# Two-layer gMLP and attention encoder on one core: later maxima transposes, one post step per key tile, bias copies on ScalarE, second weight low halves on GpSimd

## The chip, the cores and the metric

The kernel runs on one core of a Trainium2 chip. The metric is the device time of one execution in microseconds, the median of three runs. Five engines work side by side, each through its own row of instructions in order: TensorE (PE, with PEld for its weight loads), VectorE (DVE), ScalarE (ACT), GpSimd (POOL) and SyncE (SP), which issues the DMAs. TensorE's clock has two levels, 1.2 and 2.4 GHz; the profile gives the mean clock granted in a stretch as a share of the higher level.

## What is computed

x is 1 x 2048 x 1024 in float32. Two layers run one after the other, each:

```python
h = rmsnorm(x, pre_g[l])
proj = jnp.einsum('bsd,de->bse', h, w_in[l])
u_a, v_a, g_a, q, k, v, g_b = jnp.split(proj, idx, axis=-1)
# gmlp_group: layernorm of v, then per chunk of 128 positions, 8 groups of 64 channels
z = jnp.einsum('hij,bcjhd->bcihd', ws, vn) + sb.T[None, None, :, :, None]
y_a = u * z * silu(g_a)
# 8 query heads, 2 key/value heads, head_dim 64, rmsnorm of q and k, axial rotary, softmax over all 2048 keys
y_b = gqa_axial_attention(q, k, v, q_norm_g[l], k_norm_g[l], tables) * silu(g_b)
out = jnp.einsum('bse,ed->bsd', concatenate([y_a, y_b]), w_out[l])
x = x + rmsnorm(out, post_g[l])
```

## The kernel before

Large matmuls keep float32 precision by splitting each operand into a high part, rounded for TensorE, and a low part, the rest; three products (high-high, high-low, low-high) are summed in psum. All psum tiles of 128x512 share one ring of seven buffers, called "ps": a matmul that starts a tile waits until the engine that reads the tile seven allocations ago is done.

**Projections** (in the trace 0 to 620 us for layer 0, 1385 to 1985 us for layer 1). The 2048 tokens go in two halves. For each half, blocks of 256 columns of `w_in` are loaded into `w_raw` (L257), and `split_w` makes `w_hi` with an ACT copy and `w_lo` with a DVE subtraction (L267, L268), in two halves of 128x1024 each (`n=4`: d = 0 and d = 4; some first blocks are split finer, with `n=2`). Products go to `pp`; rotary products (`fc`, `fa`, L342 to L365) run on DVE and POOL; the gMLP takes `fv`, splits it into `fh` (ACT, L435) and `fl` (POOL, L436) and multiplies by the spatial weights `ws`. The spatial weights are transposed by PE, copied from psum to `wsT` (L233, two 128x512 copies a layer on DVE) and split; the bias of the gMLP comes from a small product, copied from psum to `zbias` by two 64x128 DVE copies for each of four columns c (L249, L250). Calls on PE, ACT, DVE and POOL through the helper `Pinned` (all at L84) keep the order of the program text. Calls on `nc.scalar`, `nc.vector` and `nc.gpsimd`, such as those of `split_w` and of the bias, are placed by a scheduler, which fixes each engine's row before the run.

**Attention** (620 to 1385 and 1985 to 2740 us). 32 units (4 blocks of 512 queries x 8 heads) of 16 key tiles make 512 key tiles a layer, about 1.5 us each. In key tile k the loop issues two score matmuls `sp`, two exponentials on ACT (`p_parts` high half, and `p_f`), the low half on POOL (15 of 100 on DVE), then post steps, then the jobs noted for this k by `at(k, ...)`, then some output projection matmuls `pout` ("fill"), then the `po` product of an earlier tile. The row maximum of a unit to come is found beforehand: 16 `max_step`s (a `pmax` matmul and a DVE reduction to `mx`, 681 ns) spread over `span` = 20 key tiles from `k0`, then `max_row` (the DVE reduction to `m_neg`) at `k0 + span + 1`, then `stack_max`: a PE transpose `t<-ident,m_neg`, `m_rows` by ACT and DVE, and two stores to `m_d` on SP. `load_q` of the unit, which reads `m_d`, comes 10 key tiles before the unit starts. So `mx` and `m_neg` have buffers for three units.

**Post steps.** Each finished output tile (128 tokens x 1024 columns) puts its steps into `post_queue`: 8 small DVE steps for the reciprocal root `rs_o`, two adds `o_t<-o_t,rs_o,x_r` of 128x512, a store; in layer 0, for tiles of the first half of the tokens, also two ACT squares, 8 more small steps, two DVE products `x_r` and the store `h_d`: 11 or 24 steps. The loop takes two steps per key tile from this queue. 12 tiles a layer go this way in the loop; what is left when the next tiles are loaded is issued at once by `load_part`. The last block's tiles go through a loop of its own behind the attention (L1159 on), which also takes two steps at a time.

Of the kernel before, what the change touches and what calls it, by code (L numbers as in the profile page):

```python
# [9 lines left out]
F32 = mybir.dt.float32  # L10
# [4 lines left out]
ALU = mybir.AluOpType  # L15
# [4 lines left out]
P = 128  # L20
# [5 lines left out]
HD = 64  # L26
# [12 lines left out]
def encoder(ctx: ExitStack, tc, x, w_in, w_out, pre_g, post_g, ln_a_g, ln_a_b,  # L39
            spatial_w, spatial_b, q_norm_g, k_norm_g, rope, out):  # L40
    nc = tc.nc
# [20 lines left out]
    def w_t(shape, name, dt=F32R):  # L62
        return wp.tile(shape, dt, name=name, tag="w")

    def f_t(name, n=GRP, dt=F32):
        return fp.tile([P, n], dt, name=name, tag="f")

    def row_t(name, shape=(P, D), dt=F32):
        return rowp.tile(list(shape), dt, name=name, tag="row")

    def ps_t(name):
        return psum.tile([P, GRP], F32, name=name, tag="ps", bufs=7)
# [14 lines left out]
    PE, ACT, DVE, POOL = Pinned(nc.tensor), Pinned(nc.scalar), Pinned(nc.vector), Pinned(nc.gpsimd)  # L87
# [87 lines left out]
    class Project:  # L175
# [39 lines left out]
        def spatial_weights(self):  # L215
            l = self.l
            self.lng = lay.tile([P, 4], F32, name="lng")
            nc.sync.dma_start(self.lng, ln_a_g[l].rearrange("(t p) -> p t", p=P))
            self.zbias = lay.tile([P, 4, P], F32, name="zbias")
            wsT = row_t("wsT")  # L220
            for hf in range(2):
                raw = f_t("fa")
                nc.sync.dma_start(raw.rearrange("p (g j) -> p g j", g=4),
                                  spatial_w[l, 4 * hf:4 * hf + 4].rearrange("g i j -> i g j"))
                hi = f_t("fh", dt=F32R)
                lo = f_t("fl", dt=F32R)

                def t(hf=hf, raw=raw, hi=hi, lo=lo):
                    ps = ps_t("pt")
                    for g in range(4):  # L230
                        PE.transpose(ps[:, g * P:(g + 1) * P], raw[:, g * P:(g + 1) * P], ident)
                    sl = slice(hf * GRP, (hf + 1) * GRP)
                    nc.vector.tensor_copy(wsT[:, sl], ps)  # L233
                    nc.scalar.copy(hi, wsT[:, sl])
                    nc.gpsimd.tensor_tensor(lo, wsT[:, sl], hi.bitcast(F32), ALU.subtract)
                    nc.sync.dma_start(ws_d[:, 0, sl], hi.bitcast(F32))
                    nc.sync.dma_start(ws_d[:, 1, sl], lo.bitcast(F32))
                bg.add(WS_DELAY + 2 * hf, t)
            lnb = f_t("fb")
            nc.sync.dma_start(lnb, ln_a_b[l].partition_broadcast(P))  # L240
            sb = row_t("sb_row", (1, D))
            nc.sync.dma_start(sb, spatial_b[l:l + 1].rearrange("o g i -> o (g i)"))
            for c in range(4):
                def b(c=c):
                    ps = ps_t("pt")
                    PE.matmul(ps[:, 0:2 * P], lnb[:, c * P:(c + 1) * P], wsT[:, 2 * c * P:(2 * c + 2) * P],
                              start=True, stop=False)
                    PE.matmul(ps[:, 0:2 * P], ones1, sb[:, 2 * c * P:(2 * c + 2) * P], start=False, stop=True)
                    nc.vector.tensor_copy(self.zbias[0:HD, c, :], ps[0:HD, 0:P])  # L249
                    nc.vector.tensor_copy(self.zbias[HD:P, c, :], ps[HD:P, P:2 * P])  # L250
                bg.add(WS_DELAY + 8 + 2 * c, b)

        def load_w(self, cols):
# [7 lines left out]
        def split_w(self, raw, n=4):  # L261

            hi = w_t([P, ND, WB], "w_hi")
            lo = w_t([P, ND, WB], "w_lo")
            for d in range(0, ND, n):
                sl = slice(d, d + n)
                nc.scalar.copy(hi[:, sl], raw[:, sl])  # L267
                nc.vector.tensor_tensor(lo[:, sl], raw[:, sl], hi.bitcast(F32)[:, sl], ALU.subtract)  # L268
            return hi, lo

        def hT_jobs(self, g, tail=False):
# [357 lines left out]
    def attend(l, kv, nxt):  # L629

        k_st, k_lo, _, v16 = kv
# [23 lines left out]
        def at(k, f):  # L655
            later.setdefault(k, []).append(f)
# [33 lines left out]
        def stack_max(u, pe, act, dve):  # L690
            s = state[u]
            qb, h = units[u]
            ps = ps_t("t2")
            pe.transpose(ps[0:TPG, 0:P], s.m, ident)
            for i in range(2):
                rows = small.tile([TPG, P], F16, name="m_rows", bufs=4)
                if i == 0:
                    hi = rows
                    act.activation(rows, ps[0:TPG, 0:P], AF.Copy, bias=EXP_SHIFT)
                else:  # L700
                    dve.scalar_tensor_tensor(rows, ps[0:TPG, 0:P], EXP_SHIFT, hi, ALU.add, ALU.subtract)
                nc.sync.dma_start(m_d[qb][h, i].rearrange("(t p) -> t p", p=P), rows)
# [72 lines left out]
        post_queue = []  # L775
# [225 lines left out]
        span = ((len(units) - 1) * NT - 16) // (len(units) - pre)  # L1001
# [42 lines left out]
        for u in range(pre, len(units)):  # L1044
            k0 = (u - pre) * span
            if k0 >= 8:
                at(k0 - 8, lambda u=u: load_qm(u))
            for n in range(steps):
                at(k0 + n * span // steps, lambda u=u, n=n: max_step(u, n, PE, DVE))
            at(k0 + span + 1, lambda u=u: max_row(u, DVE))  # L1050
            at(k0 + span + 3, lambda u=u: stack_max(u, PE, ACT, DVE))

        def load_gb(u):
            qb, h = units[u]
# [37 lines left out]
        for k in range(end + 4):  # L1092
            if k < total:
                u, i = k // NT, k % NT
                s = state[u]
                kv = units[u][1] // (NH // NKV)
                if i == 0 and units[u][1] % 2 == 0:
                    load_gb(u)
                ss = slice(i * P, (i + 1) * P)
                sp = ps_t("sp")  # L1100
                PE.matmul(sp, k_st[:, kv, ss], s.qs, start=True, stop=False)
                PE.matmul(sp, k_lo[0:HD + 2, kv, ss], s.q2[0:HD + 2], start=False, stop=True)
                ACT.activation(p_hi(k), sp, AF.Exp)
                ACT.activation(p_f(k), sp, AF.Exp)
                if not dve_share(k):
                    sub_lo(k, POOL)
            for _ in range(2):
                if post_queue:
                    post_queue.pop(0)()
            kb = k - 1  # L1110
            if 0 <= kb < total and dve_share(kb):
                sub_lo(kb, DVE)
            for f in later.pop(k, []):
                f()
            if k >= end:
                pop_fill((4, 5, 20)[min(k - end, 2)])
            elif fill:
                room = sum(weight(q) for q in range(k, max(k + 1, fill_to)))
                pop_fill(-(-len(fill) * weight(k) // room))
            kb = k - LAG  # L1120
            if 0 <= kb < total:
                u, i = kb // NT, kb % NT
                s = state[u]
                kv = units[u][1] // (NH // NKV)
                if i == 0:
                    s.po = ps_t("po")
                PE.matmul(s.po, v16[:, i, kv, :], p_hi(kb), start=(i == 0), stop=False)
            kb = k - LAG_LO
            if 0 <= kb < total:
                u, i = kb // NT, kb % NT  # L1130
                s = state[u]
                kv = units[u][1] // (NH // NKV)
                if i % BATCH == BATCH - 1:
                    while narrow:
                        narrow.pop(0)()
                    for n in range(i - BATCH + 1, i + 1):
                        kn = kb - i + n
                        q = n % 2 * HD
                        for c in range(0, HD, 32):
                            PE.matmul(s.po[q + c:q + c + 32], v16[:, n, kv, c:c + 32], p_lo(kn),  # L1140
                                      start=False, stop=(n >= NT - 2))
                        q = HD - q
                        PE.matmul(sums[q:q + 32], one_h, p_lo(kn), start=(n < 2), stop=(n >= NT - 2))
                        PE.matmul(sums[q + 32:q + HD], one_h, p_hi(kn), start=(n < 2), stop=(n >= NT - 2))
                if i == NT - 1:
                    finish(u, k + 1)
                    if units[u][1] == NH - 1 and u + 1 < len(units):
                        fill_to = min(k + 16 + NH * NT, total - LAST_0)
                        at(k + 16, lambda qb=units[u][0]: fill.extend(out_steps(qb)))
# [7 lines left out]
        n = 0  # L1157
# [74 lines left out]
```

## Time and profile before

| | us |
|---|---|
| median of three runs | 2775.79 (2775.23 to 2775.82) |
| profiled execution | 2771.47 |
| its span in the trace | 2769.3 |
| PE busy | 2677.1 |
| PEld busy | 1782.0 |
| DVE busy | 1896.8 |
| ACT busy | 1522.7 |
| POOL busy | 1287.0 |

The mean granted clock is 0.992. A timeline row gives the start, the time of the whole row (for "x2" that of both), the engine, the line, the operation, `out<-in`, and in brackets how long the engine had been idle ahead of it and who released it. Line numbers are those of the kernel before; in the changed kernel lines from L268 on are one higher.

### The profile page before, as it was taken

The page shows a single profiled execution, that of the slowest core. Times are in us where ns is not written, and L with a number is a line of the kernel's source. Part 1 is how long each engine was busy: PE and PEld are TensorE (multiplying, and loading weights), DVE is VectorE, ACT ScalarE, POOL GpSimd, SP SyncE. Part 2 cuts the span into 40 slices and gives each one's busy share as a digit, 9 for nine tenths or more (in the row PEclk, how much of TensorE's full clock was granted, in tenths as well). Part 3 has the DMA queues.
Part 4 walks back from the last instruction along what each step waited for, and adds up shares of the span by engine and source line. Part 5 has one row for each costly group of instructions (what it writes and reads, how often), then busy time and mean ns, then how long its engine had stood idle before and what let it go on. Part 6 is the DMA issues. An engine that isn't in the chain of part 4 may idle for free.

```text
span 2769.3 us, 48428 instructions
## 1 busy us (share of the span) xinstructions
PE 2677.1 (97%) x18230; PEld 1782.0 (64%) x18230; DVE 1896.8 (68%) x3796; ACT 1522.7 (55%) x3005; POOL 1287.0 (46%) x1080
## 2 busy tenths in 40 slices
PE   7999999999999999999999999999999999999997
PEld 6898899764444444444589989997644444444444
DVE  8862688876666776776487528888766666666664
ACT  4221432117887787787732214221288877778774
POOL 1210122007786676776632101210277767667765
PEclk9999999999999999999999999999999999999999
DMA  4424522322222232222354334333322222221313
GB/s 143 146 81 127 165 76 81 112 63 89 89 71 81 75 98 79 82 80 80 110 179 138 115 114 134 88 92 98 94 64 72 82 70 73 81 76 47 112 46 129
DMA packets 275310, 265.31 MB, mean 96 GB/s; under 512 B 19202, under 2 KB 233346, under 8 KB 275076
## 3 DMA queue, kind: packets, MB, share of 16 engines
q1 hardware_dynamic: 275076, 262.22, 30.2%
q8 instruction: 143, 2.34, 0.3%
q14 instruction: 91, 0.75, 0.1%
HBM read 177.09 MB, written 85.07 MB: 95 GB/s over the span
## 4 chain that ended last, share of the span: by engine, by line
PE 77%; DVE 11%; ACT 5%; DMA 3%; issue 2%; POOL 1%; SPq 0%; DVEq 0%; POOLq 0%; ACTq 0%
PE pp L84 27%; PE sp L84 14%; PE po L84 11%; PE pout L84 11%; PE pmax L84 7%; PE sums L84 4%; PE pt L84 2%; DVE fc L363 2%; ACT p_parts L84 2%; ACT p_f L84 2%; DMA w_raw<-in_w_in_dram 1%; DVE mx L84 1%; DVE o_t L84 1%; DVE w_lo L268 1%; ACT w_hi L267 1%
## 5 line engine op out<-in xcount | busy, mean ns | idle before, releaser
L84 POOL TENSOR_TENSOR p_parts<-p_f,p_parts 128x512 f16<-128x512 f32 x872 | 1034.9, 1205 | 404.2 <-ACT p_f L84 304.3
L84 ACT ACTIVATE p_parts<-sp 128x512 f16<-128x512 f32 x1024 | 630.0, 615 | 296.5 <-PE sp L84 289.8
L84 DVE TENSOR_REDUCE mx<-pmax 128x1 f32<-128x512 f32 x768 | 513.0, 681 | 211.9 <-PE pmax L84 209.9
L84 PE MATMUL pout<-wo,y_t 128*128 128x512 f32 x1488 | 657.1, 506 | 0.7 <-ACT p_f L84 0.3
L84 PE MATMUL po<-p_parts,v_st 128*32 128x512 f16 (+1 forms) x3072 | 639.2, 383 | 0.2
L84 ACT ACTIVATE p_f<-sp 128x512 f32<-128x512 f32 x1024 | 632.0, 617 | 0.0
L84 PE MATMUL pp<-w_hi,hT 128*128 128x256 f32 x3584 | 502.5, 290 | 16.1 <-DVE hT L310 9.7
L84 PEld LDWEIGHTS pp<-w_hi,hT 128*128 128x128 f32 x3584 | 462.0, 194 | 21.8 <-DVE hT L310 10.9
L84 PE MATMUL sp<-q_st,k_t 128*128 128x512 f16 x1024 | 390.2, 381 | 8.3 <-DVE mx L84 5.5
L84 PE MATMUL pmax<-k_t,q_m 128*128 128x512 f16 x1024 | 389.7, 382 | 7.6 <-DVE mx L84 3.2
L84 PEld LDWEIGHTS <-v_st 128*32 128x32 f16 (+1 forms) x3072 | 193.7, 96 | 309.5 <-issue 253.0
L84 PE MATMUL sp<-q,k_t 66*128 66x512 f16 x1024 | 391.0, 382 | 0.0
L84 PEld LDWEIGHTS pout<-wo,y_t 128*128 128x128 f32 x1488 | 281.3, 190 | 128.4 <-issue 8.7
L84 PEld LDWEIGHTS <-k_t 128*128 128x128 f16 (+1 forms) x2048 | 191.5, 99 | 187.7 <-issue 74.4
L468 POOL TENSOR_TENSOR fl<-fa,fh 128x512 fp32r<-128x512 f32 x32 | 43.1, 1346 | 533.3 <-ACT fh L467 489.2
L84 PE MATMUL pp<-hT,w_hi 128*128 128x512 f32 x1024 | 271.7, 413 | 0.0
L84 PE MATMUL pp<-w_lo,hT 128*128 128x256 f32 x1792 | 262.6, 290 | 0.0
L84 PE MATMUL sums<-p_parts,one_h 128*32 128x512 f16 x2048 | 242.3, 380 | 0.0
L84 PEld LDWEIGHTS pp<-w_lo,hT 128*128 128x128 f32 x1792 | 235.5, 194 | 0.9
L84 PEld LDWEIGHTS pp<-hT,w_hi 128*128 128x128 f32 x1024 | 193.4, 190 | 35.3
L683 DVE TENSOR_REDUCE mx<-pmax 128x1 f32<-128x512 f32 x256 | 172.6, 687 | 49.1 <-PE pmax L84 47.5
L84 PEld LDWEIGHTS <-q_m 128*128 128x128 f16 x1024 | 99.8, 98 | 140.2 <-issue 42.1
(161 smaller groups left out, 2790.9 us busy)
## 6 DMA issues: line engine op xcount, KB each, us to landing
w_raw<-in_w_in_dram SPq DMA_DIRECT2D x28, 1024.0 KB
y_t<-y_d SPq DMA_DIRECT2D x56, 512.0 KB
w_raw<-in_w_in_dram SPq DMA_DIRECT2D x32, 512.0 KB
x_t<-in_x_dram SPq DMA_DIRECT2D x16, 512.0 KB
z_d<-fb SPq DMA_DIRECT2D x32, 256.0 KB
gb_d<-fa SPq DMA_DIRECT2D x32, 256.0 KB
fb<-z_d SPq DMA_DIRECT2D x32, 256.0 KB
y_d<-fh SPq DMA_DIRECT2D x32, 256.0 KB
```

The source lines that it names most:

```text
L84: return tc.keep_in_program_order(call(*args, **kw))
L267: nc.scalar.copy(hi[:, sl], raw[:, sl])
L268: nc.vector.tensor_tensor(lo[:, sl], raw[:, sl], hi.bitcast(F32)[:, sl], ALU.subtract)
L363: nc.vector.tensor_tensor(t2[:, :, :, lo:lo + 16], qn[:, :, :, hi:hi + 16], tbi[:, :, 1:2, lo:lo + 16].broadcast_to([P, 2, n, 16]), ALU.mult)
L468: nc.gpsimd.tensor_tensor(lo, th, hi.bitcast(F32), ALU.subtract)
L683: dve.tensor_reduce(s.mx[:, j, c:c + 1], ps, AX.X, ALU.max)
```

## The change

Five edits: the `wsT` copies (4) and the `zbias` copies (16) move from DVE to ACT; the second half of a weight block's `w_lo` (42 of 84 subtractions of 128x1024) moves from DVE to POOL; `stack_max` is issued at `k0 + span + 5` instead of `+ 3`; the attention loop takes one post step per key tile instead of two (the loop behind it still takes two).

```diff
-                    nc.vector.tensor_copy(wsT[:, sl], ps)
+                    nc.scalar.copy(wsT[:, sl], ps)
...
-                    nc.vector.tensor_copy(self.zbias[0:HD, c, :], ps[0:HD, 0:P])
-                    nc.vector.tensor_copy(self.zbias[HD:P, c, :], ps[HD:P, P:2 * P])
+                    nc.scalar.copy(self.zbias[0:HD, c, :], ps[0:HD, 0:P])
+                    nc.scalar.copy(self.zbias[HD:P, c, :], ps[HD:P, P:2 * P])
...
-                nc.vector.tensor_tensor(lo[:, sl], raw[:, sl], hi.bitcast(F32)[:, sl], ALU.subtract)
+                engine = nc.gpsimd if n == 4 and d else nc.vector
+                engine.tensor_tensor(lo[:, sl], raw[:, sl], hi.bitcast(F32)[:, sl], ALU.subtract)
...
-            at(k0 + span + 3, lambda u=u: stack_max(u, PE, ACT, DVE))
+            at(k0 + span + 5, lambda u=u: stack_max(u, PE, ACT, DVE))
...
-            for _ in range(2):
-                if post_queue:
-                    post_queue.pop(0)()
+            if post_queue:
+                post_queue.pop(0)()
```

POOL in the first half of layer 0's tokens, before: the gMLP low parts `fl` (L436, L468) follow each other.

```order
L342 TENSOR_TENSOR fa<-fa,gain_q 128x512
L360 TENSOR_TENSOR fc<-fc,fa 128x512 x2
L436 TENSOR_TENSOR fl<-fv,fh 128x512 x8
L468 TENSOR_TENSOR fl<-fa,fh 128x512 x8
L342 TENSOR_TENSOR fa<-fa,gain_k 128x512
```

POOL at the same place now (L437 and L469 are the former L436 and L468):

```order
L361 TENSOR_TENSOR fc<-fc,fa 128x512 x2
L437 TENSOR_TENSOR fl<-fv,fh 128x512 x4
L269 TENSOR_TENSOR w_lo<-w_raw,w_hi 128x1024 x2
L437 TENSOR_TENSOR fl<-fv,fh 128x512 x4
L269 TENSOR_TENSOR w_lo<-w_raw,w_hi 128x1024 x2
L469 TENSOR_TENSOR fl<-fa,fh 128x512
L269 TENSOR_TENSOR w_lo<-w_raw,w_hi 128x1024
```

Two `w_lo` now stand between the first and the second four `fl` of L437, and single ones among those of L469; the other half of the tokens and layer 1 have the same pattern.

DVE at the post steps of one of the first output tiles in the attention of layer 0, before:

```order
L84 TENSOR_SCALAR rs_t<-rs_o,rs_m 128x1
L84 TENSOR_SCALAR rs_o<-rs_t,rs_o 128x1
L84 TENSOR_REDUCE mx<-pmax 128x1
L84 SCALAR_TENSOR_TENSOR o_t<-o_t,rs_o,x_r 128x512 x2
L84 TENSOR_REDUCE mx<-pmax 128x1 x2
```

And now:

```order
L84 TENSOR_REDUCE mx<-pmax 128x1
L84 SCALAR_TENSOR_TENSOR o_t<-o_t,rs_o,x_r 128x512
L84 TENSOR_REDUCE m_neg<-mx 128x4
L84 TENSOR_REDUCE mx<-pmax 128x1
L84 SCALAR_TENSOR_TENSOR o_t<-o_t,rs_o,x_r 128x512
L84 TENSOR_REDUCE mx<-pmax 128x1 x2
```

The two adds no longer follow each other.

ACT where the spatial weights are prepared in layer 0, before:

```order
L234 CAST fh<-wsT 128x512 x2
L267 CAST w_hi<-w_raw 128x1024 x2
L350 ACTIVATE fb<-pp 128x512 x2
L410 CAST fh<-pt 128x512 x2
L573 COPY fv<-pp 128x512 x2
```

And now:

```order
L267 CAST w_hi<-w_raw 128x1024 x2
L351 ACTIVATE fb<-pp 128x512 x2
L249 COPY zbias<-pt 64x128
L250 COPY zbias<-pt 64x128
L249 COPY zbias<-pt 64x128
L250 COPY zbias<-pt 64x128
L411 CAST fh<-pt 128x512
L249 COPY zbias<-pt 64x128
L250 COPY zbias<-pt 64x128
L411 CAST fh<-pt 128x512
L574 COPY fv<-pp 128x512
```

The bias copies of the first two columns stand ahead of the first `fh`, the others among the `fh` and `fv`.

## Rows read from the trace of the kernel before

**Rows 1.** Page, section 1: busy us (share of the span) xinstructions by engine.
```profile
PE 2677.1 (97%) x18230; PEld 1782.0 (64%) x18230; DVE 1896.8 (68%) x3796; ACT 1522.7 (55%) x3005; POOL 1287.0 (46%) x1080
```

**Rows 2.** What PE waited for: engine line, releaser, us in total, times, longest.
```profile
PE t L84 <- DVE m_neg L84: 6.3, 9, 1.1
PE sp L84 <- DVE mx L84: 5.5, 6, 1.9
PE pp L84 <- DVE zbias L250: 4.5, 2, 2.5
...
PE pmax L84 <- DVE mx L84: 3.2, 3, 1.5
```

**Rows 3.** Stretches: us, busy PE PEld DVE ACT POOL, PEclk, DMA share, GB/s.
```profile
20.00:120.00 100.00, 91.21 (x718) 87.60 (x716) 90.41 (x231) 37.09 (x78) 21.23 (x17) 0.97 0.36 111
...
620.00:1385.00 765.00, 747.24 (x5072) 357.09 (x5071) 504.03 (x899) 597.36 (x1201) 542.52 (x453) 1.00 0.26 85
```

**Rows 4.** Slices of 20 us, same columns; PEclk third from the end.
```profile
120.00:140.00 20.00, 17.53 (x127) 16.55 (x127) 14.55 (x35) 3.42 (x6) 4.29 (x3) 0.91 0.72 223
...
940.00:960.00 20.00, 18.10 (x121) 7.89 (x123) 16.21 (x36) 15.38 (x34) 13.48 (x12) 0.91 0.21 70
...
2500.00:2520.00 20.00, 18.52 (x140) 8.44 (x139) 16.23 (x30) 14.89 (x30) 14.04 (x12) 1.00 0.12 45
```

**Rows 5.** Timeline at two adds: start, us, engine, line, operation, [idle, releaser].
```profile
951.51 3.03 DVE L84 SCALAR_TENSOR_TENSOR o_t<-o_t,rs_o,x_r 128x512 f32<-128x512 f32 x2
...
955.20 0.38 PE L84 MATMUL sp<-q_st,k_t 128*128 128x512 f16 x1 [1.90 <-DVE mx L84]
```

**Rows 6.** Timeline at a transpose of row maxima.
```profile
711.94 0.16 DVE L84 TENSOR_REDUCE m_neg<-mx 128x4 f32<-128x16 f32 x1
...
712.15 0.27 PE L84 MATMUL t<-ident,m_neg 128*4 128x128 f32 x1 [1.08 <-DVE m_neg L84]
```

**Rows 7.** Timeline at a bias copy.
```profile
122.79 0.29 DVE L250 COPY zbias<-pt 64x128 f32<-64x128 f32 x1
...
123.23 2.05 PE L84 MATMUL pp<-w_hi,hT 128*128 128x256 f32 x8 [2.47 <-DVE zbias L250]
...
127.12 0.59 ACT L573 COPY fv<-pp 128x512 f32<-128x512 f32 x1 [5.73 <-DVE fc L365]
```

**Rows 8.** ACT groups: operation, shapes, count, busy us, mean ns, idle before.
```profile
L382 ACT COPY v_st<-pp 128x256 f32<-128x256 f32 x16 | 5.9, 371 | 22.5 <-PE pp L84 22.5
```

**Rows 9.** DVE groups, same columns.
```profile
L268 DVE TENSOR_TENSOR w_lo<-w_raw,w_hi 128x1024 fp32r<-128x1024 f32 x84 | 104.4, 1256 | 18.8 <-ACT w_hi L267 17.6 <-PE pp L84 0.6
```

**Rows 10.** POOL at L436: count, ns min/median/max, first and last start, shapes.
```profile
L436 POOL TENSOR_TENSOR fl<-fv,fh x32: 1284/1296/2894, 149.4 to 1840.8; 128x512 fp32r<-128x512 f32 x32
```

**Rows 11.** Timeline at the fifth low part of layer 0's first half.
```profile
178.13 2.00 ACT L267 CAST w_hi<-w_raw 128x1024 fp32r<-128x1024 f32 x2 [5.82 <-DMA w_raw<-in_w_in_dram]
...
179.76 2.36 DVE L268 TENSOR_TENSOR w_lo<-w_raw,w_hi 128x1024 fp32r<-128x1024 f32 x2
...
183.29 0.39 PE L84 MATMUL pt<-ws,fl 128*128 128x256 f32 x1 [1.29 <-POOL fl L436]
```

**Rows 12.** The same place in layer 1.
```profile
1552.14 2.35 DVE L268 TENSOR_TENSOR w_lo<-w_raw,w_hi 128x1024 fp32r<-128x1024 f32 x2
...
1555.66 0.39 PE L84 MATMUL pt<-ws,fl 128*128 128x256 f32 x1 [1.28 <-POOL fl L436]
```

**Rows 13.** The same place in the second half of layer 0.
```profile
463.36 1.05 ACT L267 CAST w_hi<-w_raw 128x1024 fp32r<-128x1024 f32 x1
...
466.68 0.28 PE L84 MATMUL pt<-ws,fl 128*128 128x256 f32 x1
```

**Rows 14.** DVE at L363, same columns.
```profile
L363 DVE TENSOR_TENSOR fc<-fc,fa x192: 208/279/1387, 54.0 to 1787.1; 128x128 f32<-128x128 f32 x128, 128x64 f32<-128x64 f32 x64
```

**Rows 15.** Timeline at the first projection.
```profile
27.20 1.22 DVE L268 TENSOR_TENSOR w_lo<-w_raw,w_hi 128x1024 fp32r<-128x1024 f32 x1
...
29.31 1.23 PE L84 MATMUL pp<-w_hi,hT 128*128 128x256 f32 x4 [4.57 <-DVE hT L310]
```

## What I predict, and why

> **What bounds the kernel now.** I read the page first: PE is busy for 2677.1 of 2769.3 us, the other engines for 46 to 68% [rows 1]. So a saving on DVE is worth only what PE waits for, and PE's idle time, about 92 us, is all that this change can win. Next the list of what PE waited for [rows 2]; the reader is to see that the largest lines behind the start are released by DVE, in small pieces: `m_neg` 6.3 us, `mx` 5.5 + 3.2, `zbias` 4.5. The table by stage [rows 3] says how full DVE is: 90.4 of 100 us early in the projections, but 504 of 765 in the attention of layer 0. In the attention DVE is late only in bursts; in those projection stretches it paces. The rows of single stalls come next, each with its part. A last view is the granted clock by slice [rows 4]: after some stalls a slice shows 0.91 where others show 1.00. In 20 us that is 0.09 x 20 = 1.8 us of work; I take 1.7 for one such dip. The profiled run took 2771.47 us, 4.3 below the median of 2775.79; I sum against the profiled one and carry the 4.3 over.
>
> **One post step per key tile.** No work is removed. Before, the two `o_t` adds of an output tile stand next to each other on DVE; now a reduction or two stand between. The pair ran 3.03 us from 951.51; reductions of `pmax` queue behind it, PE needs the psum tile that such a reduction frees, and stood 1.90 us at 955.20 [rows 5]. In all PE stood 8.7 us in nine waits for `mx`, none longer than 1.9 [rows 2]; four of them, 1.9 to 1.5 us each, lie right behind such a pair, so about 6.8. Two of those four lie in slices with 0.91 (940:960, and 1140:1160 alike), while the slices of the others show 1.00 [rows 4]: 2 x 1.7 = 3.4 us more. How much remains? A key tile lasts about 765/512 = 1.49 us, and DVE is busy for 504/765 = 66% of it, adds included. With one add of half of 3.03 in a tile beside a reduction of about 0.7, DVE falls some 0.6 us behind per tile, 1.2 over two, where the pair put it up to 3 behind; as only four of the 24 tiles' pairs gave a stall of 1.5 us or more, 1.2 should mostly fit. Ends: 3 us (stalls halve, one dip stays) and 11 (most `mx` waits and both dips). I take **-7.5**. An output tile of layer 0 with 24 steps needs 24 key tiles instead of 12 and just fits ahead of the next; its store and `h_d` write are issued some 12 tiles later on SP's queue, ahead of nothing that PE needs within them. The DVE and ACT steps move with it.
>
> **Transposes two key tiles later.** PE keeps order, so at `t<-ident,m_neg` it stands until `m_neg` is there: 9 times, 6.3 us, the longest 1.1 [rows 2]. At 712.15 it stood 1.08 us for a reduction that began at 711.94 [rows 6], queued behind other DVE work. The reduction is issued two tiles before the transpose now and four after the change; 2 x 1.49 = 3 us cover a lateness of about 1. Behind the transpose come ACT's and DVE's `m_rows`, two SP stores and the load of `q2`: they move 3 us, and the last unit's, with the load now issued one tile after the transpose, has ten tiles, some 14 us, to its use. So the wait goes; what is late next is the `mx` reduction behind it on DVE, for which PE has a few psum tiles of room. Ends: 3 (half reappears there) and 7 us (with small waits that other rows name). I take **-5.5**.
>
> **Bias copies on ScalarE.** 16 small copies of about 0.29 us [rows 7] and four `wsT` copies leave DVE, which paces there, for ACT. PE stood 2.47 us at 123.23 for the second copy of a pair, which began at 122.79 behind `rs_y` work on DVE, while ACT had been idle for 5.73 us when it went on at 127.12 [rows 7]; the like in layer 1 makes it 4.5 us in two waits [rows 2]. On ACT a 64x128 copy from psum is not in the trace; the nearest row is 128x256 at 371 ns [rows 8], so above nothing and below 0.37, I take 0.3, nearest that row. They hide beside DVE. Behind them in ACT's row wait only `fh` and `fv`. Gain: 4.5 us, less up to half for the next wait on DVE's `fc` in the same place, and the dip of the slice 120:140 (0.91 [rows 4]), 1.7. Ends 2 and 6.5; I take **-5**.
>
> **Second low halves on GpSimd.** 42 of 84 subtractions of 128x1024 leave DVE (1256 ns each [rows 9], 53 us in all). On POOL that shape is not in the trace: the nearest row is the same operation on 128x512, 1284 ns at least, 1296 median [rows 10], so twice that, 2.57 us; DVE's 1.22 for the same tile is the other bound. I take 2.55, so 42 x 2.55 = 107 us on a POOL with 21 of 100 us busy in 20:120 [rows 3]. The weights are split a block or more ahead, so PE does not wait for these halves themselves. But POOL keeps its row, and after the change two `w_lo` stand between the first and second four `fl<-fv,fh`, at four places. At the first, PE waits for `fl` already: 1.29 us at 183.29 [rows 11]. There the second high half ends at 178.13 + 2.00 = 180.13. If POOL starts at once, `w_lo` ends at 182.68, and `fl` (1.29) at 183.97 instead of 183.29: +0.7. If DVE's own half, from 179.76 and 1.22 long, is let through first, POOL starts at 180.98: `w_lo` to 183.53, `fl` to 184.82, +1.5. In layer 1, where DVE's half starts at 1552.14 as the high half ends and PE goes on at 1555.66 [rows 12], the two cases give 1552.1 + 3.84 = 1555.9, +0.3, and 1553.36 + 3.84 = 1557.2, +1.5. In the other half of the tokens the second high half ends at 464.41, or 0.4 earlier since ACT now issues both ahead of the `fh` [rows 13]; `w_lo` to 466.6 to 467.0, `fl` to 467.8 to 468.2, and PE wants it at 466.68: +1.1 to 1.5, and again in layer 1, which I take to be alike. Sum 0.7 + 0.3 + 2 x 1.1 = 3.2 to 6.0. A stall of over 2 us may bring a dip, 0 to 2 x 1.7. I take 5 + 1 = **+6**, ends 3 and 9.5.
>
> Elsewhere DVE is freed of 1.22 us per half, but a DVE operation with two sbuf inputs stands still beside a running POOL one: an `fc` product has a median of 279 ns and a maximum of 1387 [rows 14]. So a POOL subtraction can hold DVE for up to 2.55 us. About 13 of the 42 lie in the stretches that DVE paces (20:120, 340:420, 1385:1420, 1690:1780: 26 of the 84 lie there). Each then gains 1.22 or loses 2.55 - 1.22 = 1.33: -16 to +17 us on DVE, at most that on PE; I take +1, with -3 to +8. One place stands for the gain: at 29.31 PE waited 4.57 us for an `hT` that stood behind two low halves on DVE [rows 15]; one leaves (-1.2), yet the first may have to wait for POOL (+0.5). I take -0.5.
>
> **Sum.** -7.5 - 5.5 - 5 + 6 + 1 - 0.5 = -11.5, and I give back 0.5 for stalls that now end in each other: -11. 2771.5 - 11 = 2760.5, and with the 4.3 carried over **2765 us**. About 0.2%, 5.5 us, is what a measurement of this kernel can tell from no change: 2770.2 to 2781.3 is "same".
>
> **Rivals.** *A, the stalls are given back.* PE runs ahead after a removed stall and stands at the next DVE result, since no DVE work went in the attention: only a third of 18, 6, is won, and the four `fl` places and DVE take it: 2771.5 + 0 to 1, so 2776. For it: `mx` waits occur apart from pairs, too; against: DVE has a third of its time free there [rows 3].
>
> *B, POOL holds DVE* (the other side). Each of the 13 halves in DVE-paced stretches starts while products of `fc` or `hT` additions follow on DVE: 13 x 1.33 = 17 us, plus 6.0 at `fl`, plus 3.4 of dips, 26.4, against 18 won: 2775.8 + 9 = 2785. It decides from the point where over half of them start ahead of a two-input DVE operation. For it: the `fc` maximum; against: much of the DVE work there has a psum input, which a POOL operation need not hold.
>
> The row of `fc` [rows 14] shows both: 279 ns at the median, so most products ran free, and 1387 at the worst. The Trainium skill ("SBUF — State Buffer", section "Who interferes with whom") states a lock on a port pair that VectorE and GpSimd share: whichever issues first keeps it for the whole instruction, and the other blocks fully. The worst row agrees with that; by the rule at every one of the 13 halves the time would be this rival's 2785, by the median row it stays at the forecast.
>
> *C, nearly all is won.* POOL's halves fit, DVE's relief counts: -11 - 7 - 6.5 + 3 - 3 = -24.5, 2751.
>
> **How the numbers follow.** Forecast 0.53, C 0.10, A 0.23, B 0.14. Faster: forecast, C and a little of A, less the forecast's upper end: 0.63; same 0.23; slower 0.14. The forecast's own terms reach from 2753 to 2772; with A in and half of B the range is 2753 to 2781.
>
> **What would show it.** After: no PE gap over 1 us from `m_neg`; single `o_t` adds with a `mx` between and no `mx` gap over 1.2; slices without 0.91 in the attention; no `zbias` row among PE's waits, ACT's copies at about 0.3 us; PE's 1.29 us at the first `fl` place grown to 2 or more, and the same in layer 1; POOL's `w_lo` near 2.55 us and DVE 50 us less busy, or, for B, more `fc` products at 1 us and more. It is wrong if the attention of layer 0 keeps over 15 of its 17.8 idle PE us (765 - 747.24), or if the stretch 20:120 grows by more than 3 us.

## The result

| | median us | runs | ratio to the kernel before, 95% interval |
|---|---|---|---|
| before | 2773.7 | 18 | |
| changed | 2779.6 | 18 | 1.0023 (1.0016 to 1.0031) |

The change makes the kernel slower by 0.23%, about 6.4 us, where 11 us less were forecast (the three runs shown ahead of the prediction are among the 18 of before). One of the 18 took 2980.7 us, 7% above all others, and is left out of the ratio. The profiled execution of the changed kernel took 2776.92 us, with a span of 2774.7, 5.4 above that of before.

First the busy times on the page of the changed kernel, which answer to [rows 1], then what its PE waited for ([rows 2]; engine line, releaser, us in total, times, longest):

```profile
PE 2679.0 (97%) x18230; PEld 1784.8 (64%) x18230; DVE 1856.3 (67%) x3734; ACT 1525.2 (55%) x3025; POOL 1391.9 (50%) x1122
```

```profile
PE pp L84 <- DVE hT L311: 13.5, 4, 4.0
...
PE pmax L84 <- DVE mx L84: 7.3, 11, 2.3
PE pt L84 <- POOL fl L437: 7.0, 4, 2.7
...
PE pt L84 <- ACT fh L436: 4.6, 2, 2.4
...
PE pt L84 <- DVE k_t L397: 3.5, 3, 1.3
```

The reader is to see what left and what came. `zbias` (4.5), `m_neg` (6.3) and `sp` on `mx` (5.5) are gone from the top of the list, as foretold. In their place stand `fl`, which was 2.6, an `fh` that was not there, `hT` at 13.5 after 9.7, `pmax` on `mx` at 7.3 after 3.2, and the rotary result `k_t` at 3.5 after 0.4. DVE has 40 us less to do and POOL 105 more, yet PE waits for both.

The stages say where. Slices of 20 us of the changed kernel (us, busy PE, PEld, DVE, ACT, POOL, PEclk, DMA share, GB/s), two of which, 120 and 940, stand in [rows 4]:

```profile
120.00:140.00 20.00, 20.00 (x158) 18.67 (x157) 12.16 (x27) 4.85 (x11) 4.34 (x3) 1.00 0.77 245
180.00:200.00 20.00, 17.75 (x133) 17.55 (x134) 11.58 (x27) 3.26 (x6) 5.58 (x5) 0.91 0.35 107
320.00:340.00 20.00, 17.84 (x138) 17.84 (x139) 16.32 (x49) 7.69 (x20) 3.07 (x2) 0.91 0.60 194
470.00:490.00 20.00, 17.56 (x126) 16.51 (x125) 17.89 (x36) 4.87 (x8) 6.76 (x5) 0.91 0.32 93
940.00:960.00 20.00, 19.58 (x129) 9.01 (x122) 14.26 (x28) 14.90 (x31) 12.66 (x11) 1.00 0.31 96
980.00:1000.00 20.00, 17.73 (x128) 7.50 (x126) 13.54 (x19) 13.69 (x28) 14.01 (x12) 0.91 0.28 90
```

The stretches at 120 and 940 that showed 0.91 are back at 1.00; 180, 320, 470 and 980, at 1.00 before, show 0.91 now. I also matched the PE matmuls of one trace with the same ones of the other. By the start of the attention the changed kernel of layer 0 is 6.9 us late, though it had won some 5 at the bias copies; the attention of layer 0 wins 4.5 and that of layer 1 2.9; the projections of layer 1 lose 6.1, the 2.3 won at their bias copies counted in. So the projections lose what all the rest wins, and more.

What a low half on POOL does at the first `fl` place is seen in the timeline there (start, us, engine, line, operation, [idle before, releaser]), which answers to [rows 11]:

```profile
175.83 2.00 ACT L267 CAST w_hi<-w_raw 128x1024 fp32r<-128x1024 f32 x2 [6.33 <-DMA w_raw<-in_w_in_dram]
...
177.91 2.45 POOL L269 TENSOR_TENSOR w_lo<-w_raw,w_hi 128x1024 fp32r<-128x1024 f32 x1 [9.05 <-ACT w_hi L267]
178.05 4.93 DVE L430 TENSOR_SCALAR fv<-fv,mv_v,rs_y 128x512 f32<-128x512 f32 x4
...
181.34 0.50 PE L84 MATMUL pt<-ws,fh 128*128 128x256 f32 x2 [2.39 <-ACT fh L436]
...
182.75 0.40 PE L84 MATMUL pt<-ws,fl 128*128 128x256 f32 x1 [0.90 <-POOL fl L437]
```

POOL's subtraction starts 0.14 us ahead of DVE's four scalings `fv`, and these take 4.93 us where they took 1.92 before:

```profile
177.93 1.92 DVE L429 TENSOR_SCALAR fv<-fv,mv_v,rs_y 128x512 f32<-128x512 f32 x4
```

The first takes 2.58 us, 0.54 being the median: it ends just after POOL's subtraction. ACT's `fh` waits for it and PE for that, 2.39 us, then 0.90 for `fl`. In the other half of the tokens, where [rows 13] had PE go on at 466.68 without a stall:

```profile
468.39 2.39 POOL L269 TENSOR_TENSOR w_lo<-w_raw,w_hi 128x1024 fp32r<-128x1024 f32 x1 [9.33 <-ACT w_hi L267]
...
468.61 3.25 DVE L269 TENSOR_TENSOR w_lo<-w_raw,w_hi 128x1024 fp32r<-128x1024 f32 x1
...
470.74 4.72 POOL L437 TENSOR_TENSOR fl<-fv,fh 128x512 fp32r<-128x512 f32 x3
...
473.04 0.54 PE L84 MATMUL pt<-ws,fl 128*128 128x256 f32 x1 [2.44 <-POOL fl L437]
```

DVE's own half of the block, 1.18 us in [rows 11] (2.36 for two), stands still behind POOL's half and takes 3.25; then POOL's first `fl` stands still behind DVE's. And at the first `hT` of the next half, a place that the prediction did not look at:

```profile
316.27 2.36 POOL L269 TENSOR_TENSOR w_lo<-w_raw,w_hi 128x1024 fp32r<-128x1024 f32 x1 [8.41 <-ACT w_hi L267]
...
316.60 3.10 DVE L269 TENSOR_TENSOR w_lo<-w_raw,w_hi 128x1024 fp32r<-128x1024 f32 x1
...
322.16 1.48 PE L84 MATMUL pp<-w_hi,hT 128*128 128x256 f32 x8 [4.02 <-DVE hT L311]
```

DVE's half takes 3.10 instead of 1.22, the `hT` additions stand behind it, and PE waits 4.02 us, where it waited 2.13 in the kernel before:

```profile
315.65 1.22 DVE L268 TENSOR_TENSOR w_lo<-w_raw,w_hi 128x1024 fp32r<-128x1024 f32 x1
...
319.32 1.22 PE L84 MATMUL pp<-w_hi,hT 128*128 128x256 f32 x8 [2.13 <-DVE hT L310]
```

### The profile page after: what moved, and what is told of

Same layout as the page of the kernel before. It is cut to its first block, busy times and chain, and to the rows that moved or that the text cites. A ratio compares the mean times of both kernels' runs of the same rounds, so it can differ in the third digit from the quotient of the medians.

```text
span 2774.7 us, 48466 instructions
## 1 busy us (share of the span) xinstructions
PE 2679.0 (97%) x18230; PEld 1784.8 (64%) x18230; DVE 1856.3 (67%) x3734; ACT 1525.2 (55%) x3025; POOL 1391.9 (50%) x1122
## 4 chain that ended last, share of the span: by engine, by line
PE 81%; DVE 8%; ACT 5%; DMA 2%; issue 2%; POOL 1%; SPq 0%; DVEq 0%; POOLq 0%; ACTq 0%
PE pp L84 29%; PE sp L84 14%; PE po L84 11%; PE pout L84 11%; PE pmax L84 7%; PE sums L84 4%; PE pt L84 3%; DVE fc L364 2%; ACT p_parts L84 2%; DMA w_raw<-in_w_in_dram 2%; ACT p_f L84 1%; DVE mx L84 1%; DVE p_parts L84 1%; DVE o_t L84 1%; ACT w_hi L267 1%
## 5 line engine op out<-in xcount | busy, mean ns | idle before, releaser
L84 PE MATMUL pp<-w_hi,hT 128*128 128x256 f32 x3584 | 503.8, 290 | 15.5 <-DVE hT L311 13.5
L269 POOL TENSOR_TENSOR w_lo<-w_raw,w_hi 128x1024 fp32r<-128x1024 f32 x42 | 107.3, 2555 | 377.0 <-ACT w_hi L267 348.8
```

Source lines behind the costliest of these rows:

```text
L84: return tc.keep_in_program_order(call(*args, **kw))
L269: engine.tensor_tensor(lo[:, sl], raw[:, sl], hi.bitcast(F32)[:, sl], ALU.subtract)
```

## The experiments

**Each edit alone.** Four kernels, each with one edit of the change and nothing else: `span + 5`; one post step; the 20 copies on `nc.scalar`; the second low half on `nc.gpsimd`.

> Only the transposes of the row maxima are two key tiles later. Theory M (the stall moves): in the changed kernel PE stands 0.81 us for an mx reduction at 773.53, 1006.16, 2141.77 and 2369.51, just where it stood 0.9 us for m_neg before, so DVE is late there in any case: 0 to 2 us below the kernel before. Theory P (the recorded term): the m_neg stalls of 6.3 us go, 5.5 us below.

> Only one post step per key tile. Theory M: the four mx stalls of 1.5 to 1.9 us behind two adds go with their two low-clock stretches, but a new stall of about 2.3 us with a low-clock stretch comes where an x_r product and a low half on DVE meet (985.58 in the changed kernel): 4 to 7 us below the kernel before. Theory P: 7.5 us below, no new stall over 1.2 us.

> Only the wsT and zbias copies move to ScalarE. Both stalls for zbias (2.47 and 2.04 us) go, and with the first one its low-clock stretch: theory M, from the matched times of the two traces, 7 us below the kernel before (5.0 in layer 0, 2.3 in layer 1); theory P (recorded) 5 us below; rival, given back at the next fc on DVE, 0 to 2 below.

> Only the second low halves of the weight blocks move to GpSimd. Theory M: they cost about 20 us (14.8 at the four places of fl, two of them because DVE's scalings of fv stand still behind POOL's w_lo, the rest at hT and rotary products), so about 2793 us if the kernel before takes 2773.5, and the four places show PE stalls of 2.4 us or more. Theory P: 6 to 7 us above the kernel before, POOL's row being the only cause.

| edit alone | median us | ratio, 95% interval | us won (-) or lost |
|---|---|---|---|
| later transposes | 2773.3 | 0.9999 (0.9990 to 1.0009) | 0 |
| one post step | 2769.1 | 0.9983 (0.9975 to 0.9992) | -4 |
| bias copies on ACT | 2766.2 | 0.9970 (0.9959 to 0.9981) | -7 |
| low halves on POOL | 2797.6 | 1.0083 (1.0069 to 1.0097) | +24 |

Their kernel before ran at 2773.3. The low halves explain the sign, at more than three times the recorded term. The later transposes show no win alone (0, with 2.6 us either way), and PE's waits in that run tell why:

```profile
PE pmax L84 <- DVE mx L84: 7.0, 9, 1.5
...
PE sp L84 <- DVE mx L84: 4.8, 5, 1.9
...
PE sp L84 <- ACT p_f L84: 2.9, 6, 1.4
```

The 6.3 us for `m_neg` are gone, but `pmax` on `mx` rose from 3.2 to 7.0 and `sp` on `p_f` from 1.0 to 2.9. Two other rows fell, `pmax` on `p_f` from 2.3 to 1.1 and `sp` on `mx` by 0.7, so some 2.5 us of waiting are won. In the changed kernel the rows at 773 show a place to which the wait moved:

```profile
771.49 1.39 DVE L84 TENSOR_TENSOR p_parts<-p_f,p_parts 128x512 f16<-128x512 f32 x1
...
773.40 0.15 DVE L84 TENSOR_REDUCE m_neg<-mx 128x4 f32<-128x16 f32 x1
...
773.53 0.38 PE L84 MATMUL pmax<-k_t,q_m 128*128 128x512 f16 x1 [0.81 <-DVE mx L84]
```

It is the place of the former 0.90 us for `m_neg`: DVE comes late to `mx` and `m_neg` alike, since ahead of them stand `o_pair`, `den` and a low half `p_parts` at the end of a unit. PE now gets past the transpose and stands at the next `pmax`.

The single post step trades. The four stalls behind two adds are gone, but a new one has come, in the changed kernel at 985.58:

```profile
982.01 1.36 DVE L84 SCALAR_TENSOR_TENSOR x_r<-o_t,rs_o,g_row 128x512 f32<-128x512 f32 x1
...
983.29 1.64 DVE L84 TENSOR_TENSOR p_parts<-p_f,p_parts 128x512 f16<-128x512 f32 x1
...
985.58 0.59 PE L84 MATMUL pmax<-k_t,q_m 128*128 128x512 f16 x1 [2.27 <-DVE mx L84]
```

An `x_r` product and a low half follow each other without a reduction between, as the two adds did. And with this edit alone PE waits longer for `m_neg` than the 6.3 us of before; the cause stays open:

```profile
PE t L84 <- DVE m_neg L84: 9.3, 11, 1.3
```

**The three edits without the low halves.** The changed kernel with the line of `split_w` as before.

> The changed kernel without its fourth edit: all low halves stay on VectorE, the other three edits are in. If the single edits add up (0, -4.2 and -7.1 us against 2773.3), it takes 2762 us, 17 below the changed kernel: the moved low halves then cost 17 beside the other edits, against 24.3 alone. If the low halves on GpSimd relieved VectorE somewhere (rival), it is above 2768.

2757.3 us, ratio 0.9944 (0.9930 to 0.9957), 14.9 below its kernel before, and below the 2762 of the sum. Beside the other edits the low halves thus cost 6.4 + 14.9 = 21 us. Matched matmul by matmul with this kernel, the changed one is 19.1 us late at the end; it loses 3.8, 4.3, 2.0 and 4.6 us at the four places of `fl`, 14.6 in all, and 3.4 and 2.1 at the two waits of 4.02 us for `hT`, of which some comes back behind them. The three edits win 3.6 more together than the sum of the single ones, which is no more than the intervals (some 4 us either way) leave to chance.

**Where those 3.6 us come from.** Bias copies and one post step, transposes as before.

> Bias copies on ScalarE and one post step per key tile; transposes as before. If the later transposes are worth nothing beside these (as alone), 2757 us as with them; if the 3.6 us by which the three edits beat the sum of the single ones come from the transposes, 2761.

2760.2 us (0.9951, 0.9938 to 0.9963), between the two numbers. It is 12.8 us below its own kernel before, where the three edits are 14.9 below theirs: the later transposes win about 2 us beside the other two edits, and the intervals overlap. The traces say more. By the matched matmuls the attention of the two layers together is 2.4 us shorter with the later transposes than without, in this pair of kernels and in the single edit against the kernel before alike. So nothing shows that the edit is worth less alone: the profiled run of the single edit lost 9.6 us in the projections, where its code is that of before. Of the wait for `m_neg` (6.3 us before, 9.3 in the kernel with bias copies and one post step) about a third came through, not all and not nothing.

**Is it the low half on DVE in the attention?** None of the four edits; only the key tiles whose low half VectorE makes:

```diff
-            n = SHARE_0 if k < NH * NT else SHARE
-            return k * n // 100 != (k + 1) * n // 100
+            u, i = k // NT, k % NT
+            return i in (0, 9) or (i == 15 and u % 5 < 2)
```

> The kernel before, with the 77 low halves per layer that VectorE makes in the attention at key tiles 0 and 9 of each unit (and 15 of some), away from the tiles 2 to 7 in which the end of the last unit gives VectorE its o_pair, den and m_neg work. Nothing of the four edits is in. Theory M (m_neg was late because such a low half of about 1.4 us stood ahead of it): the m_neg stalls of 0.9 us go without moving any transpose, 3 to 6 us below the kernel before. Rival (the lateness is of the reductions themselves): within 1 us of it.

2760.3 us, ratio 0.9958 (0.9945 to 0.9970): 11.9 below, twice what was expected (78 low halves a layer, where before had 76). PE's wait for `m_neg` fell from 6.3 in nine to

```profile
PE t L84 <- DVE m_neg L84: 2.4, 2, 1.2
```

with every transpose where it was. `pg`'s four waits of 1.1 us left the top of the list as well. The lateness was of DVE, made by a low half next to the end of a unit, and not of the transposes.

POOL has a part in that lateness, too. How long one operation takes on DVE in the attention varies by more than two to one; the adds of the kernel before (ns min/median/max):

```profile
L84 DVE SCALAR_TENSOR_TENSOR o_t<-o_t,rs_o,x_r x48: 739/1293/1769, 868.1 to 2727.1; 128x512 f32<-128x512 f32 x48
```

The 38 adds that began while a POOL operation was running took 1.36 us in the mean, the 10 others 0.74; of DVE's 152 low halves `p_parts`, 82 began so and took 1.08, the others 0.69. `o_pair`, with one input in psum, took 0.69 either way. POOL's own low halves run beside the pair at 951.51, the low half at 771.49 and the two operations at 982; so each of these operations holds some 0.7 us of work, and the rest of its time is standing still beside POOL. The edits moved where this happens and did not end it: 43 low halves of DVE take over 1 us in the kernel before, and 43 with the low halves shifted.

**Post steps by their size.** Small steps two per key tile, adds and `x_r` products alone and never beside a low half:

```diff
-            for _ in range(2):
-                if post_queue:
-                    post_queue.pop(0)()
+            n = 0
+            while post_queue and n < 2:
+                wide = post_queue[0] in wides
+                if wide and (n or (0 <= k - 1 < total and dve_share(k - 1))):
+                    break
+                post_queue.pop(0)()
+                n += 2 if wide else 1
```

> The kernel before with another rule for post steps: small steps still two per key tile, an add or x_r product alone in its tile, and never in a tile in which VectorE also makes a low half. Theory M (the stall at 979 in the single edit comes from an x_r product of 1.4 us next to a low half of 1.6): no mx stall over 1.2 us is left and about 8 us are won, 2765; if the product and the low half do not matter together, it comes out as the single edit did, 2769.

2767.9 us (0.9986, 0.9977 to 0.9995), no better than the single post step. The stall at 979 is gone, but 1.47 us for `mx` remain at 956.64 and at 2320.43, where the two adds fall in neighbouring key tiles with no reduction between. The expected 2765 did not come. One step per key tile parts the adds and also puts them in other key tiles; how much of its win is the one and how much the other stays open.

**Which low halves cost.** The low halves alone on GpSimd, with some blocks taken back by `self.split_w(raw, far=False)` and

```diff
-                engine = nc.gpsimd if n == 4 and d else nc.vector
+                engine = nc.gpsimd if n == 4 and d and far else nc.vector
```

> As the low halves alone on GpSimd (2797.6 us, 24.3 above the kernel before), but the eight second halves of the two blocks that are split while the gMLP low parts fl are made stay on VectorE; 34 remain on GpSimd, and the eight fl of a half follow each other again. Theory M: the four places gave 14 to 16.6 us, so 2781 to 2784, and PE waits for fl as before, twice 1.3 us. If the harm is spread evenly over the 42, 2793.

2779.7 us (1.0027, 1.0017 to 1.0037): 7.6 above its kernel before, so eight of 42 halves made 17 of the 24 us, as much as expected, and PE's row for `fl` is that of before:

```profile
PE pt L84 <- POOL fl L437: 2.6, 2, 1.3
```

The rest was looked for at `hT`:

> As the run with 34 low halves on GpSimd (2779.7 us), but that of the k/v block, split just ahead of the next half's first hT, stays on VectorE too; 32 remain on GpSimd. In that run PE stood 4.02 us for hT at 323.88 and 1698.15, against 2.13 before, since VectorE's own low half waits for GpSimd's of the same block. Theory M: both go back to 2.13, 4 us or more are won, 2773 to 2776. If the hT wait has another cause, 2780.

> As the run with 34 low halves on GpSimd (2779.7 us), but the first block of q, four times, keeps both low halves on VectorE; 30 remain on GpSimd. The run that took back the k/v block changed the wrong one: a w_lo still ran on POOL for 2.36 us from 319.22 there, and the row of hT came after it. Theory M: that one belongs to the q block, the hT waits of 4.02 us at about 324 and 1698 go back to 2.13, and 4 to 6 us are won: 2774 to 2776. If the wait has another cause than the low half on POOL, 2780 and 4.02 again.

2780.7 (1.0024, 1.0014 to 1.0035) and 2779.4 us (1.0022, 1.0013 to 1.0031): nothing. Both took the wrong block; in both the row of `hT` still shows 4.02 or 4.03 us. The second did take away a stall of 2.20 us for `hT` at 49, and its median did not move. Matched with the run of 34, its matmuls lose 1.2 us at 29, where the first `hT` wait is longer, and come 4.8 us earlier from 49 to 57; 1.1 of that is gone by 77 and 2.4 more by 134, where its slice 120:140 shows a granted clock of 0.91 and that of the other run 1.00. Whether DVE's work or the clock took the gain back, one trace of each kernel cannot tell.

> As the run with 34 low halves on GpSimd (2779.7 us), but the second block of q keeps both low halves on VectorE; 30 remain on GpSimd, and the last w_lo ahead of the next half's hT leaves POOL's row. Theory M: VectorE's own half no longer stands behind it, both hT waits of 4.02 us (about 324 and 1698) return to 2.13, and what follows them too: 3.8 us and up to 1.7 for a low-clock stretch, 2774 to 2776. If VectorE's work, not this wait, sets the time of that stretch (rival, as the last run hints, where a stall at 49 went and the time did not), the waits return to 2.13 and the time stays at 2779.

2773.6 us (1.0001, 0.9992 to 1.0010). With the second block of q back on VectorE the row at `hT` reads

```profile
318.20 0.98 PE L84 MATMUL pp<-w_hi,hT 128*128 128x256 f32 x6 [2.13 <-DVE hT L311]
```

and the time is that of the kernel before. The stall at 49 is gone here as well: matched with the run of 34, 5.0 us are won from 49 to 57 and 3.2 and 3.4 at the two `hT` waits, of which 5.6 is left at the end. So 12 of the 42 halves (eight at `fl`, four of the second q block) cost all of the 24 us, and the 30 others on GpSimd come out even, within 2.5 us. That is a sum: the waits for `zbias`, 4.5 us, are gone in this kernel though its bias copies are still on DVE, and mostly at the same places PE now waits for rotary products:

```profile
PE pp L84 <- DVE fc L359: 4.2, 3, 2.1
```

**What beats both.** The three edits, and the low halves of the attention moved within the unit:

> The three edits without the moved low halves (2757.3 us), and the low halves of the attention on VectorE at key tiles 0, 9 and sometimes 15 of a unit, as in the run with that alone. Theory M: the stalls that are left in the attention of that kernel (k = 103, 142, 250, 263, 302 and so on, some 13 us, and one low-clock stretch) all have such a low half within the last four key tiles, so most go: 2745 to 2749. Rival: what the transposes and the post steps won is the same time, and it stays above 2753.

> Bias copies on ScalarE and the low halves of the attention shifted within the unit; transposes and post steps as before. The two touch different stages, so the sum of the single runs: 2772.7 - 7.1 - 11.9 = 2754 us. It is at or below the three edits (2757.3) if DVE's low halves, not the place of the transposes or the post steps, are what PE waits for in the attention.

2742.1 us for the first, ratio 0.9887 (0.9874 to 0.9901), 1.1% below the kernel before; 2754.5 (0.9931, 0.9918 to 0.9943) for the second, the sum of its two parts. The first is below the 2745 to 2749 expected: 30.8 us below its kernel before, where its parts, 14.9 and 11.9, add up to 26.8. The attention of layer 0, whose 17.8 idle PE us stood in [rows 3], has 11.8 in the first:

```profile
620.00:1385.00 765.00, 753.21 (x5129) 365.69 (x5127) 500.02 (x924) 601.58 (x1218) 552.68 (x460) 1.00 0.29 92
```

Of the stalls of over 0.6 us for DVE's reductions there, none is left.

## Why the prediction was wrong

The step that failed is the fourth term, "second low halves on GpSimd", +6.5 with what lies elsewhere, where the runs show 21 beside the other edits and 24 alone.

- *The places were right, their price was not.* About 17 of the 24 us lie at the four `fl` places, and 14.6 of the 19.1 in the changed kernel. The working followed POOL's row only: when the second high half is done, when `w_lo` ends, when `fl`. It let DVE be in POOL's way, but not POOL in DVE's: neither the `fv` scalings ahead of `fh` nor DVE's own half of the block. Each place cost 3.7 to 4.5 us by the matched matmuls of the run with this edit alone, where 0.3 to 1.5 were put down. Most of the rest lies at the `hT` of the next half, where the prediction put down nothing. Some of it is the low clock: 180:200 and 470:490 show 0.91, counted as 0 to 3.4 in the sum and taken as 1.
- *The two-input rule was too narrow.* The prediction said that DVE operations with two sbuf inputs stand still beside POOL. The scaling of `fv` has one such tensor, and it stood still too: 545 ns at the median, 2591 at the most, against 1530 at the most before.

```profile
L430 DVE TENSOR_SCALAR fv<-fv,mv_v,rs_y x32: 534/545/2591, 145.3 to 1835.1; 128x512 f32<-128x512 f32 x32
```

The Trainium skill ("SBUF — State Buffer", section "Who interferes with whom") names `tensor_scalar` among the operations that can take the shared port pair. This trace agrees, with 2591 against 545 ns. The prediction cited that section for the lock and left this part of it out.
- *What DVE won was given back.* 42 halves at 1256 ns are 53 us. The other 42 went to 1697 ns, 18.5 us more, where a block's two halves meet, as at 316 and 468; the `fv` scalings went from 666 to 853 ns in the mean. DVE is 40 us less busy, bias copies and `wsT` included.

```profile
L269 DVE TENSOR_TENSOR w_lo<-w_raw,w_hi 128x1024 fp32r<-128x1024 f32 x42 | 71.3, 1697 | 20.8 <-ACT w_hi L267 19.7 <-PE pp L84 0.6 <-issue 0.4
```

- *Rival B had the mechanism and for the most part the wrong place.* It said that POOL holds DVE, with 13 halves in the stretches that DVE paces. It is 12 halves, ahead of `fv`, of DVE's half and of `hT`. The four `fl` places lie outside those stretches, of the `hT` waits those at 49 and 1695 inside. Products `fc` of 1 us or more, B's sign, went from 40 to 42 only, the longest from 1.39 to 2.48 us.
- *The signs looked elsewhere.* Neither sign of being wrong came: the attention of layer 0 keeps 14.2 idle PE us (765 - 750.84), and 20:120 grew by 2.0 us by the matched matmuls. DVE is 40 us less busy, not 50, and PE's wait at the first `fl` place came as 2.39 us for `fh` and 0.90 for `fl`.
- *The duration was right.* 2555 ns per POOL half, 2.55 forecast.

```profile
L269 POOL TENSOR_TENSOR w_lo<-w_raw,w_hi 128x1024 fp32r<-128x1024 f32 x42 | 107.3, 2555 | 377.0 <-ACT w_hi L267 348.8 <-PE t L84 20.1 <-DVE o_t L84 7.8
```

The other terms: **bias copies**, -5 forecast, -7 measured; the copies take 0.26 us on ACT (0.3 forecast), both stalls and the low clock at 120:140 went, and nothing took their place. **One post step**, -7.5 forecast, -4 measured; the mechanism was right at the four places, and the step "1.2 should mostly fit" missed that an `x_r` product may meet a low half, 2.27 us and a stretch at 0.91, and that `m_neg` comes later, 3.0 us. It took half of 3.03 us for an add, which takes 0.74 where POOL is idle. **Later transposes**, -5.5 forecast, 0 (2.6 either way) by the median alone, about -2 beside the others and -2.4 in the attention by the traces; what was wrong is "so the wait goes". The wait goes, but the reason of the lateness stays, and PE meets it at the next `pmax`. The prediction named this as what comes next and gave PE "a few psum tiles of room" without a row for it. Rival A, stalls given back, was thus right for much of this edit, for a part of the post steps, and wrong for the bias copies.

The single runs add up to 24.3 - 0 - 4.2 - 7.1 = +13, against +6.4 measured for the whole. The 6.6 between them are 3.6 that the three edits win together beyond their sum and 3 by which the low halves cost less beside them; both are of the size of the intervals, and which of it is more than chance stays open. That 2779.6 still lies in the stated range, 2753 to 2781, is owed to the weight of the rivals A and B in it: the forecast's own terms end at 2772.

## What to carry to other kernels

Before moving an operation from DVE to POOL, list what DVE has to do in the same 2.5 us, and what waits for that: here 12 moved subtractions out of 42 cost 24 us and the other 30 bought nothing. A DVE operation that looks long may be a short one standing still beside POOL: compare it with its own shortest run. A stall of an engine that works in order names the place where it stood, not the cause; moving the waiting instruction back moves much of the stall, while taking the late work away (a low half of 1.4 us ahead of the reductions) ended it, for 12 us. Run edits of one change alone: two of these four helped clearly, by 4 and 7 us, a third by some 2 in the attention, and the fourth cost more than all of them won.

## What the runs showed of the hardware

A DVE scaling with one sbuf tensor of 128x512 took 2.58 us beside a POOL subtraction of 2.45 that had begun 0.14 us earlier, against 0.54 at the median. A DVE subtraction of 128x1024 took 3.10 us beside a POOL one of 2.36 that had begun 0.33 us earlier, against 1.22. Each lost 1.9 to 2.0 of the 2.0 to 2.3 us for which POOL's still ran. DVE's adds `o_t` and low halves in the attention were longer beside POOL by 0.6 and 0.4 us in the mean, `o_pair` with one input in psum by nothing.

In slices that hold a PE stall of 1.9 us ([rows 5]) to 4.0 us (the `hT` at 322.16) the granted clock is 0.91: part of the slice ran at the lower level, 1.2 GHz. Not every such stall has one, and for the same code that differs between executions: the wait for `zbias` in layer 1 is 2.04 us in the kernel before, where the slice 1490:1510 shows 1.00, and 2.07 us in the run with the low halves of the attention shifted and nothing else changed, where it shows 0.83.
